# The low parts of the branch projections' weights: made by accumulating transfers in place of VectorE's subtraction

## The chip, the cores and the metric

One core of a Trainium2 chip runs the whole kernel. The metric is the device time of one execution in microseconds, as the median of the runs shown.

## The reference

One layer of a hybrid decoder, 256 rows of width 2048, all in float32. One input projection feeds three causal mixers (a gated linear recurrence, a windowed softmax attention, a short gated convolution). Each mixer's output `o_a`, `o_b`, `o_c` (256 x 1024) is projected to width 2048, weighted by a sigmoid gate that is itself a projection of the input, and the sum goes through one output projection and a layer norm:

```
u = x @ w_in[l]
...
y_a = (o_a.astype(x.dtype) * jax.nn.silu(a_g)) @ w_proj_hgrn[l]
...
y_b = (o_b * jax.nn.silu(b_g)) @ w_proj_attn[l]
...
y_c = (o_c * jax.nn.silu(c_g)) @ w_proj_conv[l]
merged = jax.nn.sigmoid(m_a) * y_a + jax.nn.sigmoid(m_b) * y_b + jax.nn.sigmoid(m_c) * y_c
y = merged @ w_out[l]
x = layer_norm(ALPHA * x + y, ln_g[l], ln_b[l])
```

The change lies in the weights of `y_a`, `y_b` and `y_c`.

## The kernel before

Every product is made from rounded operands in TensorE's float32r format. A weight `w` is split into a high part `hi`, which is `w` rounded to float32r, and a low part `lo = w - hi`; an activation is split the same way. A product is the sum of three matmuls: activation high by `hi` (L140), activation low by `hi` (L141), activation high by `lo` (L142). Columns-major products do the same with two instructions (L147, L148).

Weights come in granules of 1024 KB (128 partitions x 2048 numbers). `load_granule` (L103) takes one of three `raw` buffers and issues the load from SyncE's queue; a load waits until the buffer's last readers are done. `gemm` (L152) walks over the granules and splits each in two halves of 128 x 1024 with `split_w` (L108): ScalarE's copy writes `hi` (L111), VectorE's subtraction writes `lo` (L112). There are four `hi` and four `lo` buffers, so a half is split when TensorE has finished the half four places ahead of it. A half then feeds twelve matmuls of 128 x 512 in `rows` (L138), two k-steps by two row blocks by three.

The last third of the kernel is the loop over `d` (four column blocks of 512) and over the three branches. For each pair it makes the gate `rows512(mc + d)` (four granules, eight halves), its sigmoid `sg` on ScalarE (L630, one for each row block), then the branch projection `gemm(a[wp][d], outs[br], NC, "rows")` (two granules, four halves), and multiplies and adds with VectorE (L634, L635, L637). So a branch takes twelve halves, and there are twelve branches. After each `d` the merged block is transposed for the output projection (the task `turn`). The order on each engine is set by a scheduler that places instructions by the waits that it expects; GpSimd (POOL) has a queue of its own for transfers that it issues in software.

Of the kernel before, what the change touches and what calls it, by code (L numbers as in the profile page):

```python
# [10 lines left out]
F32R = mybir.dt.float32r  # L11
U8 = mybir.dt.uint8
AF = mybir.ActivationFunctionType
ALU = mybir.AluOpType
AX = mybir.AxisListType

P = 128
# [3 lines left out]
NC = 512  # L21
# [15 lines left out]
HALF = 1024  # L37
# [11 lines left out]
def hybrid_kernel(ctx, tc, a, out):  # L49
    nc = tc.nc  # L50
# [4 lines left out]
    hip = ctx.enter_context(tc.tile_pool(name="hip", bufs=4))  # L55
    lop = ctx.enter_context(tc.tile_pool(name="lop", bufs=4))
# [7 lines left out]
    def t8(shape, name, dt=F32):  # L64
        return w8.tile(shape, dt, tag="w8", name=name)

    def t4(shape, name, dt=F32):
        return w4.tile(shape, dt, tag="w4", name=name)
# [7 lines left out]
    def f32(ap):  # L76
        return ap.bitcast(F32)


    xs = [t8([P, 4, 2, T], f"xs{i}", F32R) for i in range(4)]  # L80

    def split_to(dst, src):

        nc.scalar.copy(out=dst[:, :, 0], in_=src)
        nc.vector.tensor_sub(out=dst[:, :, 1], in0=src, in1=f32(dst[:, :, 0]))

    def load_x(k0, n):
        xr = t4([P, n, T], f"xr{k0}")
        nc.sync.dma_start(out=xr, in_=a["xT"][:, k0 : k0 + n])
        return xs[k0 // 4][:, k0 % 4 : k0 % 4 + n], xr  # L90
# [4 lines left out]
    def pump(n=1):  # L95
        while n and tasks:
            try:
                next(tasks[0])
                n -= 1
            except StopIteration:  # L100
                tasks.pop(0)

    def load_granule(src):  # L103
        raw = rawp.tile([P, 2, HALF], F32, tag="raw", name="raw")
        nc.sync.dma_start(out=raw, in_=src.rearrange("p (s n) -> p s n", s=2))
        return raw

    def split_w(r, hi=None, lo=None):  # L108
        hi = hi if hi is not None else hip.tile([P, HALF], F32R, tag="hi", name="hi")
        lo = lo if lo is not None else lop.tile([P, HALF], F32R, tag="lo", name="lo")  # L110
        nc.scalar.copy(out=hi, in_=r)  # L111
        nc.vector.tensor_sub(out=lo, in0=r, in1=f32(hi))  # L112
        return hi, lo

    def first_granule(src, k0, pieces):

        raw = rawp.tile([P, 2 * HALF], F32, tag="raw", name="raw")
        loaded = []
        at = 0
        for n in pieces:  # L120
            x = load_x(k0 + at, n)
            c = slice(at * NC, (at + n) * NC)
            nc.sync.dma_start(out=raw[:, c], in_=src[:, c])
            loaded.append((x, c))
            at += n
        halves = []
        for x, c in loaded:
            split_to(*x)
            if c.start % HALF == 0:
                halves.append((hip.tile([P, HALF], F32R, tag="hi", name="hi"), lop.tile([P, HALF], F32R, tag="lo", name="lo")))  # L130
            w = slice(c.start % HALF, c.start % HALF + c.stop - c.start)
            split_w(raw[:, c], *[y[:, w] for y in halves[-1]])
        return halves

    def accumulators():
        return [accp.tile([P, NC], F32, tag="acc", name="acc") for _ in range(2)]

    def rows(acc, xk, hi, lo, ts, first, last):  # L138

        nc.tensor.matmul(out=acc, lhsT=xk[:, 0, ts], rhs=hi, start=first, stop=False)  # L140
        nc.tensor.matmul(out=acc, lhsT=xk[:, 1, ts], rhs=hi, start=False, stop=False)  # L141
        nc.tensor.matmul(out=acc, lhsT=xk[:, 0, ts], rhs=lo, start=False, stop=last)  # L142

    def columns(acc, xk, hi, lo, first, last):

        if not first:
            nc.tensor.matmul(out=acc[:, :T], lhsT=lo, rhs=xk[:, 0], start=False, stop=False)  # L147
        nc.tensor.matmul(out=acc, lhsT=hi, rhs=xk, start=first, stop=last)  # L148
        if first:
            nc.tensor.matmul(out=acc[:, :T], lhsT=lo, rhs=xk[:, 0], start=False, stop=False)  # L150

    def gemm(src, xs, n, major, first=None):  # L152


        acc = accumulators()
        per = HALF // n
        kt = src.shape[0] * 2 * per
        k = 0
        for g in range(src.shape[0]):
            if first:  # L160
                halves = first_granule(src[g], k, first[g])
            else:
                raw = load_granule(src[g])
            for s in range(2):
                hi, lo = halves[s] if first else split_w(raw[:, s])
                for j in range(per):
                    xk = xs[k // 4][:, k % 4]
                    for b in range(2):
                        c = slice(b * P, b * P + P)
                        if major == "rows":  # L170
                            w = slice(j * n, j * n + n)
                            rows(acc[b][:, :n], xk, hi[:, w], lo[:, w], c, k == 0, k == kt - 1)
                        else:
                            w = slice(j * n + b * P, j * n + b * P + P)
                            columns(acc[b], xk, hi[:, w], lo[:, w], k == 0, k == kt - 1)
                    k += 1
                pump()
        return acc

    def rows512(c, first=None):  # L180
        return gemm(a["w_rows"][c], xs, NC, "rows", first)

    def columns256(c):
        return gemm(a["w_cols"][c], xs, T, "columns")
# [359 lines left out]
    outs = {"a": [], "b": [], "c": []}  # L544
# [7 lines left out]
    first = ((1, 1, 2), (2, 2), (2, 2), (2, 2))  # L552

    for hf in range(2):
        v = rows_out(rows512(AI + hf, None if hf else first), "va")
        q = t4([P, 4, T], "qa")
        for u in range(2):
            acc = columns256(AQ + 2 * hf + u)
# [15 lines left out]
    conv(0)  # L574
    load_bias(C)
    acc = gemm(a["w_cols"][BV], xs, T, "rows")
    vb = t4([P, 2, 2, KVH * DH], "vb", F32R)
    vb = [vb[:, i] for i in range(2)]
# [3 lines left out]
    acc = columns256(BK)  # L582
# [5 lines left out]
    for w in range(2):  # L588
        r = slice(64 * w, 64 * w + 64)
        nc.scalar.copy(out=kz[0][r, :, w], in_=kr[r])  # L590
        nc.vector.tensor_sub(out=kz[1][r, :, w], in0=kr[r], in1=f32(kz[0][r, :, w]))
    for hf in range(2):
        gate = t4([P, 4, T], "gb")
        for u in range(2):
            acc = columns256(BG + 2 * hf + u)
# [5 lines left out]
        for u in range(2):  # L601
            acc = columns256(BQ + 2 * hf + u)
# [12 lines left out]
    def turn(m):  # L615
        dst = t8([P, 4, 2, T], "m", F32R)
        ms.append(dst)
        yield
        for i, ps in transpose_pairs([[m[:, t, c * P : c * P + P] for t in range(2)] for c in range(4)], "mT"):
            split_to(dst[:, i : i + 2], ps)  # L620
            yield

    branches = ((MA, "w_proj_hgrn", "a"), (MB, "w_proj_attn", "b"), (MC, "w_proj_conv", "c"))
    for d in range(4):
        m = t4([P, 2, NC], "merged")
        for n, (mc, wp, br) in enumerate(branches):
            acc = rows512(mc + d)
            sg = t4([P, 2, NC], "sg")
            for t in range(2):
                nc.scalar.activation(out=sg[:, t], in_=acc[t], func=AF.Sigmoid)  # L630
            acc = gemm(a[wp][d], outs[br], NC, "rows")
            for t in range(2):
                if n:
                    nc.vector.tensor_mul(out=sg[:, t], in0=acc[t], in1=sg[:, t])  # L634
                    nc.vector.tensor_add(out=m[:, t], in0=m[:, t], in1=sg[:, t])  # L635
                else:
                    nc.vector.tensor_mul(out=m[:, t], in0=acc[t], in1=sg[:, t])  # L637
        tasks.append(turn(m))
# [41 lines left out]
    for n in range(3):  # L680
        acc = gemm(a["w_out"][n], ms, NC, "rows")
# [3 lines left out]
    for g in range(4):  # L685
        raw = load_granule(a["w_out"][3, g])
# [7 lines left out]
    for t, at, n in ((0, 0, NC), (1, 0, T), (1, T, T)):  # L694
        acc = accp.tile([P, NC], F32, tag="acc", name="acc")[:, :n]
        for k in range(KT):
            hi, lo = parts[k // 2]
# [94 lines left out]
```

## Time and profile before

| | us |
|---|---|
| median of 2 runs | 1026.2 (1025.85 to 1026.55) |
| the profiled execution's own time | 1026.14 |
| its span, first to last instruction | 1024.3 |
| TensorE busy | 1009.3 |
| VectorE busy | 656.9 |
| ScalarE busy | 516.8 |
| GpSimd busy | 32.4 |

Matmul times overlap in the trace (one is listed with 0.39 us and the next starts 0.23 us behind it), so the pace of TensorE is read from the starts. "Idle before" in a group is the time in which the engine had nothing to do ahead of those instructions, and what ended it. A transfer's time "to landing" runs from its issue to the semaphore that tells of its end.

### The profile page before, as it was taken

To read this page: it belongs to the slowest core of one execution; us is meant where nothing else is said; L and a number is where in the kernel's file an instruction comes from. 1 tells how busy PE (TensorE), PEld (TensorE's weight loads), DVE (VectorE), ACT (ScalarE), POOL (GpSimd) and SP (SyncE) were. 2 spreads that over 40 slices of the span, in tenths; PEclk is the share of its full clock that TensorE was granted. 3 is DMA by queue.
4 is the path that set the end of the run, shared out by engine and by line. 5 is a ranking of instruction groups with operands and counts; after the bars stand their busy time and mean duration, and the time that the engine had idled before them with its cause. 6 is when DMAs were issued, how large, how long until landed. Compare 5 with 4: busy or idle time off the path is not lost.

```text
span 1024.3 us, 13046 instructions
## 1 busy us (share of the span) xinstructions
PE 1009.3 (99%) x5214; PEld 855.4 (84%) x5214; DVE 656.9 (64%) x810; ACT 516.8 (50%) x702; POOL 32.4 (3%) x32
## 2 busy tenths in 40 slices
PE   8999999999999999999999999999999999999995
PEld 5888888888988888888888888888888888888885
DVE  6557788689855777777764455545554555545666
ACT  5546577656564665646554434444444434444441
POOL 1000000210010000000000000000000000000003
PEclk9999999999999999999999999999999999999998
DMA  8655545354455545444455555555455556665442
GB/s 324 242 194 177 205 136 180 137 189 144 165 196 182 191 156 200 166 168 144 168 199 203 179 194 205 173 197 205 170 200 202 180 193 237 254 248 193 177 164 83
DMA packets 30253, 192.60 MB, mean 188 GB/s; under 512 B 3776, under 2 KB 4576, under 8 KB 8176
## 3 DMA queue, kind: packets, MB, share of 16 engines
q1 hardware_dynamic: 28368, 184.85, 50.9%
q10 hardware_dynamic: 1152, 4.72, 1.3%
q0 software_dynamic: 672, 2.20, 0.7%
q8 instruction: 41, 0.67, 0.3%
q14 instruction: 20, 0.16, 0.0%
HBM read 189.63 MB, written 2.12 MB: 187 GB/s over the span
## 4 chain that ended last, share of the span: by engine, by line
PE 97%; DMA 1%; DVE 1%; SPq 0%; ACT 0%; issue 0%
PE acc L148 24%; PE acc L142 19%; PE acc L140 19%; PE acc L141 19%; PE acc L147 11%; PE lev L385 1%; DMA raw<-in_w_rows 1%; PE sc L454 1%; PE pvb L497 1%; PE acc L150 1%; PE pT L487 1%; PE pv L406 0%; PE mT L259 0%; PE lev L375 0%; DVE xres L677 0%; DVE xres L675 0%
## 5 line engine op out<-in xcount | busy, mean ns | idle before, releaser
L112 DVE TENSOR_TENSOR lo<-raw,hi 128x1024 fp32r<-128x1024 f32 (+1 forms) x341 | 414.9, 1220 | 291.5 <-ACT hi L111 290.5
L111 ACT CAST hi<-raw 128x1024 fp32r<-128x1024 f32 (+1 forms) x341 | 356.7, 1048 | 388.2 <-PE acc L141 264.2
L148 PE MATMUL acc<-xs,hi 128*128 128x512 f32 x1056 | 371.9, 396 | 0.0
L147 PE MATMUL acc<-xs,lo 128*128 128x256 f32 x990 | 278.4, 281 | 0.0
L148 PEld LDWEIGHTS acc<-xs,hi 128*128 128x128 f32 x1056 | 197.0, 188 | 43.7
L140 PE MATMUL acc<-hi,xs 128*128 128x512 f32 (+1 forms) x544 | 210.5, 387 | 2.3 <-ACT hi L111 2.3
L142 PE MATMUL acc<-lo,xs 128*128 128x512 f32 (+1 forms) x544 | 208.4, 384 | 0.4 <-DVE lo L112 0.3
L141 PE MATMUL acc<-hi,xs 128*128 128x512 f32 (+1 forms) x544 | 208.7, 384 | 0.0
L147 PEld LDWEIGHTS acc<-xs,lo 128*128 128x128 f32 x990 | 186.8, 189 | 2.2
L140 PEld LDWEIGHTS acc<-hi,xs 128*128 128x128 f32 x544 | 102.5, 188 | 24.5 <-ACT hi L111 4.4
L142 PEld LDWEIGHTS acc<-lo,xs 128*128 128x128 f32 x544 | 102.2, 188 | 21.3 <-DVE lo L112 1.2
L141 PEld LDWEIGHTS acc<-hi,xs 128*128 128x128 f32 x544 | 102.6, 189 | 19.8
L188 ACT COPY rest<-acc 128x256 f32<-128x256 f32 x66 | 24.3, 373 | 46.2 <-PE acc L148 45.3
L140 PE MATMUL acc<-hi,m 128*128 128x512 f32 (+1 forms) x120 | 45.2, 376 | 0.0
L142 PE MATMUL acc<-lo,m 128*128 128x512 f32 (+1 forms) x120 | 45.0, 375 | 0.0
L141 PE MATMUL acc<-hi,m 128*128 128x512 f32 (+1 forms) x120 | 45.0, 375 | 0.0
L142 PEld LDWEIGHTS acc<-lo,m 128*128 128x128 f32 x120 | 22.6, 188 | 4.1
L140 PEld LDWEIGHTS acc<-hi,m 128*128 128x128 f32 x120 | 22.6, 188 | 4.0
L141 PEld LDWEIGHTS acc<-hi,m 128*128 128x128 f32 x120 | 22.6, 188 | 4.0
L140 PE MATMUL acc<-hi,oa 128*128 128x512 f32 x64 | 24.9, 389 | 0.0
L141 PE MATMUL acc<-hi,oa 128*128 128x512 f32 x64 | 24.9, 389 | 0.0
L142 PE MATMUL acc<-lo,oa 128*128 128x512 f32 x64 | 24.9, 389 | 0.0
(187 smaller groups left out, 912.1 us busy)
## 6 DMA issues: line engine op xcount, KB each, us to landing
raw<-in_w_cols SPq DMA_DIRECT2D x68, 1024.0 KB, 4.8
raw<-in_w_rows SPq DMA_DIRECT2D x60, 1024.0 KB, 4.7
raw<-in_w_out SPq DMA_DIRECT2D x16, 1024.0 KB, 4.8
raw<-in_w_proj_hgrn SPq DMA_DIRECT2D x8, 1024.0 KB, 4.7
raw<-in_w_proj_attn SPq DMA_DIRECT2D x8, 1024.0 KB, 4.7
raw<-in_w_proj_conv SPq DMA_DIRECT2D x8, 1024.0 KB, 4.7
raw<-in_w_rows SPq DMA_DIRECT2D x7, 512.0 KB, 8.9
bias<-bias_dr POOLq DMA_DIRECT2D x2, 1024.0 KB, 6.1
```

What stands on the lines that cost most here:

```text
L111: nc.scalar.copy(out=hi, in_=r)
L112: nc.vector.tensor_sub(out=lo, in0=r, in1=f32(hi))
L140: nc.tensor.matmul(out=acc, lhsT=xk[:, 0, ts], rhs=hi, start=first, stop=False)
L141: nc.tensor.matmul(out=acc, lhsT=xk[:, 1, ts], rhs=hi, start=False, stop=False)
L142: nc.tensor.matmul(out=acc, lhsT=xk[:, 0, ts], rhs=lo, start=False, stop=last)
L147: nc.tensor.matmul(out=acc[:, :T], lhsT=lo, rhs=xk[:, 0], start=False, stop=False)
L148: nc.tensor.matmul(out=acc, lhsT=hi, rhs=xk, start=first, stop=last)
L150: nc.tensor.matmul(out=acc[:, :T], lhsT=lo, rhs=xk[:, 0], start=False, stop=False)
L188: nc.scalar.copy(out=rest[p], in_=acc[p, T:])
L385: nc.tensor.matmul(out=ps[:, o : o + 64], lhsT=kk[:, hd, t * P : t * P + P], rhs=qc[:, hd, t * 64 : t * 64 + 64], start=True, stop=True)
L454: nc.tensor.matmul(out=ps[:, o_ : o_ + 2 * nk], lhsT=q[:, 2 * g + x, m, blk * P : blk * P + P], rhs=kz[n][:, hf, :, 0:nk], start=(i == 0), ...
L487: nc.tensor.transpose(out=ps[:, x * P : x * P + P], in_=s[:, x // 2, x % 2, j * P : j * P + P], identity=C["ident"])
```

## The change

In the twelve branch projections alone, `split_w` is replaced by `split_by_dma`. ScalarE writes the negated rounded weight into `lo`; a transfer issued by GpSimd then adds the raw weight onto it in place (raw and `lo` both lie in SBUF); ScalarE writes `hi` as before. All other products keep `split_w`. Lines behind the new function stand 9 lower than before.

```diff
+    def split_by_dma(r):
+
+        hi = hip.tile([P, HALF], F32R, tag="hi", name="hi")
+        lo = lop.tile([P, HALF], F32R, tag="lo", name="lo")
+        nc.scalar.mul(out=lo, in_=r, mul=-1.0)
+        nc.gpsimd.dma_start(out=lo, in_=r, accum_op=ALU.add)
+        nc.scalar.copy(out=hi, in_=r)
+        return hi, lo
...
-    def gemm(src, xs, n, major, first=None):
+    def gemm(src, xs, n, major, first=None, split=split_w):
...
-                hi, lo = halves[s] if first else split_w(raw[:, s])
+                hi, lo = halves[s] if first else split(raw[:, s])
...
-            acc = gemm(a[wp][d], outs[br], NC, "rows")
+            acc = gemm(a[wp][d], outs[br], NC, "rows", split=split_by_dma)
```

Two places show how the instructions stand. The first is ScalarE at the first attention projection (d = 0): four halves, with the two sigmoids of its gate between them. Before:

```order
L111 CAST hi_5281<-raw_5279 128x1024 [waits DMAHW1_49,DVE_49,PE_49]
L111 CAST hi_5297<-raw_5279 128x1024 [waits DVE_49,PE_49]
L111 CAST hi_5315<-raw_5313 128x1024 [waits DMAHW2_49,DVE_49,PE_49]
L630 ACTIVATE sg_5274<-acc_5136 128x512 [waits PE_49]
L111 CAST hi_5331<-raw_5313 128x1024 [waits DVE_49,PE_49]
L630 ACTIVATE sg_5274<-acc_5137 128x512 [waits PE_49]
L111 CAST hi_5355<-raw_5353 128x1024 [waits DMAHW3_49,DVE_49,PE_49]
```

Each half has one instruction here; VectorE takes the rest of its split. ScalarE there in the changed kernel, where `lo` (L119) is the new multiplication by -1 and the names' numbers are four higher:

```order
L121 CAST hi_5285<-raw_5283 128x1024 [waits DMAHW1_49,DVE_49,PE_49]
L119 ACTIVATE lo_5286<-raw_5283 128x1024 [waits DMASW6_49,PE_49]
L121 CAST hi_5302<-raw_5283 128x1024 [waits DVE_49,PE_49]
L119 ACTIVATE lo_5303<-raw_5283 128x1024 [waits DMASW7_49,PE_49]
L121 CAST hi_5321<-raw_5319 128x1024 [waits DMAHW2_49,DVE_49,PE_49]
L119 ACTIVATE lo_5322<-raw_5319 128x1024 [waits DMASW0_49,PE_49]
L639 ACTIVATE sg_5278<-acc_5140 128x512 [waits PE_49]
L121 CAST hi_5338<-raw_5319 128x1024 [waits DVE_49,PE_49]
L639 ACTIVATE sg_5278<-acc_5141 128x512 [waits PE_49]
L119 ACTIVATE lo_5339<-raw_5319 128x1024 [waits DMASW1_49]
L111 CAST hi_5363<-raw_5361 128x1024 [waits DMAHW3_49,PE_49,Activation_49]
```

The new instruction stands behind the half's `hi`; that of the fourth half stands behind both sigmoids, and `hi` of the next half (`hi_5363`) behind that.

The second place is SyncE's queue there: the two granules of the projection and the three that follow. Before, the loads wait for VectorE (DVE) as the last reader of the buffer:

```order
L105 DMA raw_5279<-in_w_proj_attn 128x2048 [waits DMAHW6_49,DVE_49]
L105 DMA raw_5313<-in_w_proj_attn 128x2048 [waits DMAHW7_49,DVE_49]
L105 DMA raw_5353<-in_w_rows 128x2048 [waits DMAHW0_49,DVE_49]
L105 DMA raw_5387<-in_w_rows 128x2048 [waits DMAHW1_49,DVE_49]
L105 DMA raw_5421<-in_w_rows 128x2048 [waits DMAHW2_49,DVE_49]
```

All five wait for the same two kinds of event. In the changed kernel the loads that take over the projection's two buffers wait for accumulating transfers instead (DMASW is the software queue's semaphore):

```order
L105 DMA raw_5283<-in_w_proj_attn 128x2048 [waits DMAHW6_49,DVE_49]
L105 DMA raw_5319<-in_w_proj_attn 128x2048 [waits DMAHW7_49,DVE_49]
L105 DMA raw_5361<-in_w_rows 128x2048 [waits DMAHW0_49,DVE_49]
L105 DMA raw_5395<-in_w_rows 128x2048 [waits DMASW3_49,DMAHW1_49,DMASW2_49,Activation_49]
L105 DMA raw_5429<-in_w_rows 128x2048 [waits DMASW5_49,DMAHW2_49,DMASW4_49,Activation_49]
```

`raw_5395` and `raw_5429`, the loads behind the projection's granules, no longer wait for VectorE but for two accumulating transfers each. On GpSimd nothing stood between the second bias transfer of the attention (L435) and the layer norm (L667); the 48 transfers `lo<-raw` stand there now, in the order of the halves.

## Rows read from the trace of the kernel before

**Rows 1.** The page of the kernel before: busy time, and the chain that ended last.
```profile
PE 1009.3 (99%) x5214; PEld 855.4 (84%) x5214; DVE 656.9 (64%) x810; ACT 516.8 (50%) x702; POOL 32.4 (3%) x32
...
PE 97%; DMA 1%; DVE 1%; SPq 0%; ACT 0%; issue 0%
```

**Rows 2.** Stretches of the span: busy time by engine, granted clock, share of DMA engines, GB/s.
```profile
core 0: us, PE busy (x) PEld busy (x) DVE busy (x) ACT busy (x) POOL busy (x), PEclk, DMA share, GB/s
0.00:545.00 545.00, 540.87 (x3089) 465.89 (x3090) 398.97 (x552) 320.10 (x492) 23.71 (x24) 1.00 0.52 184
545.00:900.00 355.00, 355.00 (x1579) 293.89 (x1578) 184.72 (x172) 149.71 (x157) 0.00 (x0) 1.00 0.57 201
900.00:1024.00 124.00, 113.40 (x550) 95.66 (x548) 73.16 (x87) 46.96 (x53) 8.67 (x8) 0.97 0.47 169
```

**Rows 3.** Groups of ScalarE in the branch projections' stage, 545 to 900 us.
```profile
L111 ACT CAST hi<-raw 128x1024 fp32r<-128x1024 f32 x129 | 135.9, 1053 | 190.8 <-PE acc L141 189.1 <-DVE lo L112 1.7
L630 ACT ACTIVATE sg<-acc 128x512 f32<-128x512 f32 x22 | 13.2, 598 | 13.3 <-PE acc L142 13.3
```

**Rows 4.** Groups of VectorE in 560 to 900 us, different shapes apart.
```profile
L112 DVE TENSOR_TENSOR lo<-raw,hi 128x1024 fp32r<-128x1024 f32 x124 | 151.9, 1225 | 159.8 <-ACT hi L111 159.8
```

**Rows 5.** ScalarE in order of time around the first attention projection (576 to 590 us).
```profile
start us, us, engine line op out<-in xcount [idle before <-releaser]
...
576.21 1.05 ACT L111 CAST hi<-raw 128x1024 fp32r<-128x1024 f32 x1 [1.67 <-PE acc L141]
578.93 1.05 ACT L111 CAST hi<-raw 128x1024 fp32r<-128x1024 f32 x1 [1.67 <-PE acc L141]
581.65 1.05 ACT L111 CAST hi<-raw 128x1024 fp32r<-128x1024 f32 x1 [1.67 <-PE acc L141]
583.91 0.60 ACT L630 ACTIVATE sg<-acc 128x512 f32<-128x512 f32 x1 [1.21 <-PE acc L142]
584.41 1.04 ACT L111 CAST hi<-raw 128x1024 fp32r<-128x1024 f32 x1
585.35 0.60 ACT L630 ACTIVATE sg<-acc 128x512 f32<-128x512 f32 x1
587.09 1.05 ACT L111 CAST hi<-raw 128x1024 fp32r<-128x1024 f32 x1 [1.14 <-PE acc L141]
```

**Rows 6.** TensorE in order of time there: where the projection's first half begins.
```profile
576.01 0.39 PE L142 MATMUL acc<-lo,xs 128*128 128x512 f32 x1
576.24 0.39 PE L140 MATMUL acc<-hi,xs 128*128 128x512 f32 x1
...
584.17 0.39 PE L142 MATMUL acc<-lo,xs 128*128 128x512 f32 x1
584.40 0.39 PE L140 MATMUL acc<-hi,ob 128*128 128x512 f32 x1
584.62 0.39 PE L141 MATMUL acc<-hi,ob 128*128 128x512 f32 x1
584.85 0.39 PE L142 MATMUL acc<-lo,ob 128*128 128x512 f32 x1
...
587.57 0.39 PE L142 MATMUL acc<-lo,ob 128*128 128x512 f32 x1
```

**Rows 7.** One weight load of 1024 KB: its issue, and DMA in 575.8 to 580.8 us (40 slices).
```profile
575.83 5.77 SPq L105 DMA_DIRECT2D raw<-in_w_rows  x2
...
DMA  0000000590409019199691996939499440000000
...
q1 hardware_dynamic: 144, 1.05, 59.6%
...
raw<-in_w_rows SPq DMA_DIRECT2D x1, 1024.0 KB, 4.7
```

**Rows 8.** VectorE's low parts and the loads that they release, in order of time.
```profile
577.29 1.23 DVE L112 TENSOR_TENSOR lo<-raw,hi 128x1024 fp32r<-128x1024 f32 x1 [1.50 <-ACT hi L111]
580.02 1.23 DVE L112 TENSOR_TENSOR lo<-raw,hi 128x1024 fp32r<-128x1024 f32 x1 [1.50 <-ACT hi L111]
582.74 1.23 DVE L112 TENSOR_TENSOR lo<-raw,hi 128x1024 fp32r<-128x1024 f32 x1 [1.49 <-ACT hi L111]
585.48 1.23 DVE L112 TENSOR_TENSOR lo<-raw,hi 128x1024 fp32r<-128x1024 f32 x1 [1.52 <-ACT hi L111]
...
581.27 0.33 SPq L105 DMA_DIRECT2D raw<-in_w_rows  x1
```

**Rows 9.** The software queue's 1024 KB transfer (bias), issued at 300.22 us: DMA share by stretch.
```profile
300.22 0.96 POOL L435 DMA_DIRECT2D bias<-bias_dr  x1
...
300.20:301.70 1.50, 1.50 (x11) 1.29 (x10) 1.41 (x6) 0.30 (x1) 0.97 (x2) 1.00 0.00 0
301.70:303.00 1.30, 1.30 (x11) 1.17 (x10) 1.30 (x4) 0.78 (x1) 0.00 (x0) 1.00 0.74 205
303.00:306.30 3.30, 3.30 (x22) 2.89 (x22) 3.09 (x5) 1.95 (x5) 0.00 (x0) 1.00 1.03 364
```

**Rows 10.** The page of the kernel before: DMA issues, size of one, median us from issue to landing.
```profile
raw<-in_w_proj_hgrn SPq DMA_DIRECT2D x8, 1024.0 KB, 4.7
...
bias<-bias_dr POOLq DMA_DIRECT2D x2, 1024.0 KB, 6.1
...
oh<-in_onehot POOLq DMA_DIRECT2D x1, 48.0 KB, 3.1
...
rb<-in_rel_bias POOLq DMA_DIRECT2D x1, 2.0 KB, 3.1
```

## The prediction

> **What bounds the kernel now.** I read the page's busy times first, then the stretches of the span, then the engines in order of time around one branch projection. The page shows TensorE busy for 1009.3 of 1024.3 us and the chain that ended last made of TensorE for 97% [rows 1]. The stretches show that the branch projections' stage has no gap at all: 355.00 us busy of 355, at a granted clock of 1.00, with VectorE at 184.7 us, ScalarE at 149.7 us and the DMA engines at 0.57 [rows 2]. So nothing that VectorE is spared can shorten this stage: a gain is excluded, and the only question is whether the new `lo` comes late.
>
> In order of time, `hi` of a half is written 8.2 us ahead of its first matmul: 576.21 us for the half that TensorE begins at 584.40 [rows 5, 6]. That lead is three halves of TensorE's time, since a half can be split only when the half four places ahead of it has left its buffer (its last matmul with `lo` starts at 576.01 us [rows 6]). One half takes TensorE 2.72 us, the distance between the first `lo` matmuls of two halves, 584.85 and 587.57 [rows 6]. ScalarE works 1.05 us of each 2.72 and waits 1.67 for TensorE [rows 5].
>
> **The change part by part.**
>
> *Removed:* 48 subtractions (12 projections x 2 granules x 2 halves) of 1225 ns [rows 4], 58.8 us of VectorE. It has 170 us idle in the stage; worth 0.
>
> *Added on ScalarE:* 48 multiplications of 128x1024 into float32r. The nearest row is the cast of the same shape, 1053 ns [rows 3], so 50.5 us of ScalarE against 205 us idle. By halves: 2.1 us of each 2.72, and at the fourth half two sigmoids of 0.60 us besides [rows 5]. The next half's `hi` starts at 587.09 us now; my times below end ScalarE's work at 587.05, so it is not delayed. Worth 0. If the multiplication took twice as long, about 1 us of the lead would go.
>
> *Added on GpSimd:* 48 transfers. GpSimd has nothing else in the stage (0.00 us busy [rows 2]); the one software transfer of 1024 KB kept it 0.96 us [rows 9], under the 2.72 between two halves. Nothing useful is queued behind a transfer that waits.
>
> *Added on the DMA engines:* 48 x 512 KB, summed in place. The trace has no such transfer. I put its time from issue to landing as 1.5 + s + 0.6 us. The 1.5 is the software transfer's stretch from its issue to the first byte, in which the DMA share is 0.00 [rows 9]. The 0.6 is the weight load's tail: issued at 575.83, its last busy slice ends at 579.9 and it lands 4.7 us after the issue [rows 7]. s is the time in which the 16 engines move the half. A load of 1024 KB fills them for 59.6% of 5.0 us = 2.98 us [rows 7]. So the bounds of s are 1.5 us, if adding costs what copying 512 KB costs, and 4.5 us, if reading both operands and writing one cost three passes one after the other. I take **s = 3.0 us**: in a load, reading and writing the same bytes overlap, and the adding transfer has to read two streams of 512 KB, as many bytes as a load.
>
> A price by a page alone: the Trainium skill, in "Collectives: The Full Stack", section "The bandwidth ceiling: the fold count and why AG ≠ RS ≠ AR", says that the adding step runs at half the copying one's rate since it reads two sources (62.28 against 32.35 GB/s, a ratio of 1.93). By it s would be an estimated 2.9 us and the time an estimated 1053 us; no run here shows it yet.
>
> Now the four halves of the projection at 584.40 us, by the order in the changed kernel (`hi`, then the multiplication, then the transfer):
>
> First half: `hi` from 576.21, multiplied by 578.3, transfer issued. Bytes move 579.8 to 582.8; the load issued at 575.83 is off the engines by 579.9 [rows 7]. Landed 583.4. TensorE wants this `lo` at 584.85 [rows 6]: 1.4 us to spare.
>
> Second half: `hi` at 578.93 [rows 5], issue 581.1, bytes 582.6 to 585.7, landed 586.3, wanted at 587.57: 1.3 us to spare.
>
> Here the first granule's buffer comes free, and SyncE issues the load that waits for it, at 586.3; before it was issued at 581.27, behind VectorE's subtraction of 580.02 [rows 8]. Its bytes start 0.9 us later (the seven empty slices of 0.125 us in [rows 7]), at 587.2, and need 3.0 us of the engines.
>
> Third half: `hi` at 581.65, issue 583.8, bytes from 585.3. Wanted at 584.85 + 2 x 2.72 = 590.29.
>
> Fourth half: `hi` at 584.41 between the sigmoids, sigmoid until 585.95 [rows 5], multiplied by 587.0, issue 587.05, bytes from 588.5. Wanted at 593.01.
>
> From 585.3 on the engines never rest: 0.4 us are left of the second half, then 3.0 of the third, 3.0 of the load, 3.0 of the fourth. While the software transfer and a load ran together in 303.0 to 306.3 us they moved 364 GB/s at a share of 1.03 [rows 9], no more than 1.05 MB in 2.98 us, or 352 GB/s [rows 7], so they share and do not add. All is moved at 585.3 + 9.4 = 594.7, and the fourth half, begun last, lands at 595.3. TensorE waits 595.3 - 593.0 = **2.3 us per projection** (part of it at the third half already; the total is the same).
>
> Do the later loads add to it? The load issued at 586.3 has landed by 595.3 at the latest. The cast that needs it ran two halves behind 587.09 [rows 5], at 592.5, and moves by under 3 us; TensorE wants that half at 584.40 + 6 x 2.72 = 600.7, and cast and subtraction take 2.3 us. The load behind the fourth half is issued at 595.3 and lands by about 601; its half is wanted at 606.2. Both hold, so each projection starts afresh after eight halves of its gate.
>
> **Sum:** 12 x 2.3 = 27.6 us. Against the profiled execution's own 1026.14 us (span 1024.3; the median of the runs is 1026.2, the same within 0.1) that is **1054 us**, 2.7% slower. Under 2% either way (about 20 us) counts as no change here.
>
> **The rivals.**
>
> *Hidden.* The adding transfer costs what a copy does, s = 1.5: the second half lands at 584.7, the load's bytes run from 585.6, the fourth half's bytes from 588.5 share with the load's last 1.2 us and are through at 591.3, landed 591.9 against 593.01. No wait: 1026 us. Working the same sum at s = 2.0 gives 592.9, so the rival holds up to there; a small wait, under 2% in all, holds to about s = 2.8. For it: 0.43 of the DMA engines' time is free in the stage [rows 2], and an adder in the data's way need not slow it. Against: two operands have to be read. The Trainium skill, "DMA: Bandwidth & Descriptors", section "Anatomy of one DMA — SWDGE (gpsimd) path", gives 2.0 us plus the bytes at 436 GB/s for a software transfer: an estimated 3.2 us for a half, and by that rule nothing waits and the time stays at an estimated 1026 us. The only plain software transfer here, 1024 KB in 6.1 us beside a load [rows 9, 10], is slower than the 4.4 us of that rule.
>
> *Overrun.* Summing is slower than reading, s = 4.5 or more. Then the transfers queue behind each other, since one comes each 2.72 us: from 579.8 the engines owe 4 x 4.5 + 3.0 = 21.0 us, done at 600.8, landed 601.4, a wait of 8.4 us per projection: 12 x 8.4 = 101 us, 1127 us. At s = 6 it is 14.4 per projection, 1199 us. For it: nothing in the trace shows how fast the engines add. Against: an adding step that keeps pace with its reads needs no more than 3.0.
>
> *It does not do what it says*, as the transfer might be broken up or a subtraction stay. The order shows 48 whole transfers of 128x1024 and no VectorE subtraction in the projections, so I leave it 2 in 100.
>
> **How the numbers follow.** Forecast (s from 2.0 to 3.8) 0.44, hidden 0.27, overrun 0.27, other 0.02. The range reaches from the hidden case, 1025, to the overrun at s = 4.5, 1130, and leaves out the longer overruns. Of the forecast's cases about a quarter (s under 2.8) stays within 2%: same 0.27 + 0.11 = 0.38; slower 0.60; faster 0.02, for which I know no mechanism.
>
> **What the profile after would show.** Right: 48 transfers on the software queue of 512 KB that land in 5 to 8 us, the fourth of each projection later than the first; about 28 us of TensorE idle in the stage, at the line of the `lo` matmul (L151 there), released by a transfer, two per projection at most; the weight loads behind a projection issued some 5 us later; ScalarE's multiplication at 1.05 us. Wrong: landings under 4.5 us and no idle time (hidden), or landings over 8 us that grow through the four halves (overrun). It would also be wrong if the granted clock fell after the waits, or if the weight loads and not `lo` became late.

## The result and the profile after

The changed kernel takes 1084.9 us (median of 2 runs, 1083.4 to 1086.3) against 1026.2 us before: a ratio of 1.057, with a 95% interval of 1.054 to 1.060. It is 58.7 us slower. The profiled execution took 1083.38 us, with a span of 1081.6. (A ratio is taken over the executions within 1.5% of the same kernel's fastest; for the fifth experiment below, whose times scatter, it is therefore smaller than the ratio of the medians.)

The page of the changed kernel, with the lines that answer to [rows 1] and [rows 10], and the groups that are new:

```profile
span 1081.6 us, 13234 instructions
...
PE 1030.7 (95%) x5214; PEld 867.4 (80%) x5214; DVE 598.8 (55%) x762; ACT 562.1 (52%) x750; POOL 73.9 (7%) x80
...
PEclk9999999999999999999999999999999999899998
DMA  8655544453554554445588688778778778996542
...
PE 63%; issue 16%; DMA 16%; DVE 2%; POOL 2%; ACT 0%; SPq 0%; POOLq 0%; ACTq 0%; DVEq 0%
...
L120 POOL DMA_DIRECT2D lo<-raw x48 | 41.5, 865 | 530.8 <-ACT lo L119 502.3
...
L119 ACT ACTIVATE lo<-raw 128x1024 fp32r<-128x1024 f32 x48 | 50.7, 1056 | 0.0
...
L151 PE MATMUL acc<-lo,ob 128*128 128x512 f32 x64 | 28.3, 441 | 12.6 <-DMA lo<-raw 12.6
L151 PE MATMUL acc<-lo,oc 128*128 128x512 f32 x64 | 27.3, 427 | 11.9 <-DMA lo<-raw 11.9
L151 PE MATMUL acc<-lo,oa 128*128 128x512 f32 x64 | 27.2, 425 | 11.4 <-DMA lo<-raw 11.4
...
lo<-raw POOLq DMA_DIRECT2D x48, 512.0 KB, 5.0
```

TensorE is busy for 1030.7 us where it was for 1009.3, with the same 5214 instructions, and idle for 1081.6 - 1030.7 = 50.9 us where it was for 15.0. So of the 57.3 us by which the span grew, **35.9 us are idle time, and for 21.4 us the same instructions are busy for longer**. VectorE is relieved by 58.1 us (656.9 to 598.8) and the multiplication costs ScalarE 1056 ns each, close to the 1053 forecast. The chain, 97% TensorE before, has 16% of DMA and 16% of "issue" in it. The three groups of `lo` matmuls of the projections carry the idle time, 11.4 to 12.6 us each, put down to the transfers; these sum to the 35.9 us. The transfers' median landing is 5.0 us: I had forecast 5.1 for one that shares with nothing.

The branch projections' stage by stretches, answering to [rows 2]: the granted clock is 0.96 where it was 1.00, and the DMA engines' share 0.79 where it was 0.57.

```profile
core 0: us, PE busy (x) PEld busy (x) DVE busy (x) ACT busy (x) POOL busy (x), PEclk, DMA share, GB/s
...
545.00:900.00 355.00, 327.73 (x1389) 266.64 (x1387) 113.39 (x110) 169.37 (x179) 34.61 (x40) 0.96 0.79 224
```

In order of time, around the projection that [rows 5, 6 and 8] show before. It begins 4.82 us later here (589.22 in place of 584.40), since one projection has been through already. GpSimd's four transfers, the load that the second one's landing releases, and TensorE at the fourth half:

```profile
583.33 0.86 POOL L120 DMA_DIRECT2D lo<-raw  x1 [27.89 <-ACT lo L119]
586.05 0.86 POOL L120 DMA_DIRECT2D lo<-raw  x1 [1.86 <-ACT lo L119]
588.77 0.86 POOL L120 DMA_DIRECT2D lo<-raw  x1 [1.86 <-ACT lo L119]
592.01 0.86 POOL L120 DMA_DIRECT2D lo<-raw  x1 [2.37 <-PE acc L150]
```

```profile
591.29 0.33 SPq L105 DMA_DIRECT2D raw<-in_w_rows  x1
```

```profile
597.60 0.39 PE L150 MATMUL acc<-hi,ob 128*128 128x512 f32 x1
601.17 0.50 PE L151 MATMUL acc<-lo,ob 128*128 128x512 f32 x1 [3.17 <-DMA lo<-raw]
...
602.39 0.63 PE L149 MATMUL acc<-hi,ob 128*128 128x512 f32 x1
602.82 0.63 PE L150 MATMUL acc<-hi,ob 128*128 128x512 f32 x1
...
605.38 0.39 PE L150 MATMUL acc<-hi,xs 128*128 128x512 f32 x1
605.61 0.40 PE L151 MATMUL acc<-lo,xs 128*128 128x512 f32 x1
```

The four transfers landed 4.9, 5.1, 5.0 and **9.1 us** after their issues at 583.33 to 592.01. The load went out at 591.29, 5.2 us later against TensorE's course than the 581.27 of [rows 8]. So the fourth transfer, issued 0.7 us behind the load, landed at 601.1, and the matmul that wants its `lo` at 597.83 started at 601.17. Then the matmuls follow each other by 0.43 us in place of 0.23, for some 3.5 us. The stretches say why: the DMA engines are full up to 598, TensorE does nothing from 598.0 to 601.1, and the granted clock of the next stretch is 0.61, a mean of 1.00 at its start and the lower of the two levels (0.50, 1.2 GHz) behind it.

```profile
589.20:598.00 8.80, 8.79 (x39) 6.94 (x37) 2.45 (x2) 4.61 (x6) 1.30 (x2) 1.00 1.00 223
598.00:601.10 3.10, 0.00 (x0) 0.00 (x0) 1.23 (x1) 1.04 (x1) 0.00 (x0) 1.00 0.58 114
601.10:605.00 3.90, 3.83 (x11) 3.02 (x12) 0.69 (x1) 0.18 (x1) 0.00 (x0) 0.61 0.67 231
```

What the engines moved meanwhile, 591 to 602 us:

```profile
DMA  9999499794879999989976799999999410000000
...
q0 software_dynamic: 257, 0.92, 45.2%
q1 hardware_dynamic: 144, 1.05, 34.6%
...
lo<-raw POOLq DMA_DIRECT2D x1, 512.0 KB, 9.1
```

The software queue filled the 16 engines for 45.2% of these 11 us and the loads' queue for 34.6%: 8.8 us of work on all engines between 591 and 600, for the rest of the third transfer, the load and the fourth. The load's 1.05 MB took 3.8 us of that (34.6% of 11; 3.8 to 4.2 by the packets of all twelve projections); alone they took 2.98 [rows 7]. The two queues hardly mixed here. From 593.5 to 596.5 us the view of the DMA queues lists the loads' queue alone:

```profile
q1 hardware_dynamic: 103, 0.84, 99.2%
```

The load's first bytes moved at 593.1, when the third transfer was nearly through, and the fourth transfer's at 596.9, when the load was. That is 4.9 us after its issue, and 4.3 to 5.2 in the twelve projections; the first three transfers' bytes moved 1.4 to 1.7 us after theirs.

All twelve projections look like this: first, second and third transfers land in 4.5 to 6.0 us, the fourth in 8.4 to 9.9, and TensorE pauses once in each, for 2.45 to 3.98 us. With ten of the twelve pauses the clock fell. One of these ten stretches at the lower level, and the sum over all ten:

```profile
601.96:605.37 3.41, 3.41 (x9) 2.64 (x8) 0.87 (x2) 0.55 (x1) 0.00 (x0) 0.50 0.86 305
...
sum 37.52, PE 36.35 PEld 28.46 DVE 12.03 ACT 4.79 POOL 0.00; mean PE 3.63 PEld 2.85 DVE 1.20 ACT 0.48 POOL 0.00
```

TensorE was busy for 36.35 us at half the clock, so the clock cost about 18.2 of the 21.4 us. Of the rest some 2 us come from the counting: before a pause a matmul counts with its listed 0.39 us and not with the 0.23 to the next start, which is 12 x 0.16. The last 1.3 us were not assigned.

### The profile page after: what moved, and what is told of

Same layout as the page of the kernel before. It is cut to its first block, busy times and chain, and to the rows that moved or that the text cites. A ratio compares the mean times of both kernels' runs of the same rounds, so it can differ in the third digit from the quotient of the medians.

```text
span 1081.6 us, 13234 instructions
## 1 busy us (share of the span) xinstructions
PE 1030.7 (95%) x5214; PEld 867.4 (80%) x5214; DVE 598.8 (55%) x762; ACT 562.1 (52%) x750; POOL 73.9 (7%) x80
## 4 chain that ended last, share of the span: by engine, by line
PE 63%; issue 16%; DMA 16%; DVE 2%; POOL 2%; ACT 0%; SPq 0%; POOLq 0%; ACTq 0%; DVEq 0%
PE acc L157 23%; PE acc L156 11%; DMA lo<-raw 10%; PE acc L151 9%; PE acc L149 8%; PE acc L150 8%; DMA raw<-in_w_proj_attn 2%; DMA raw<-in_w_proj_hgrn 2%; POOL lo L120 2%; DMA raw<-in_w_proj_conv 1%; DVE lo L112 1%; PE lev L394 1%; PE sc L463 1%; PE pvb L506 1%; PE acc L159 1%
## 5 line engine op out<-in xcount | busy, mean ns | idle before, releaser
L112 DVE TENSOR_TENSOR lo<-raw,hi 128x1024 fp32r<-128x1024 f32 (+1 forms) x293 | 356.0, 1219 | 367.7 <-ACT hi L111 366.8
L111 ACT CAST hi<-raw 128x1024 fp32r<-128x1024 f32 (+1 forms) x293 | 305.9, 1047 | 374.1 <-PE acc L150 215.8
L149 PEld LDWEIGHTS acc<-hi,xs 128*128 128x128 f32 x544 | 104.0, 191 | 25.1 <-ACT hi L111 4.0
L151 PEld LDWEIGHTS acc<-lo,xs 128*128 128x128 f32 x544 | 103.2, 190 | 21.4 <-DVE lo L112 0.9
L150 PEld LDWEIGHTS acc<-hi,xs 128*128 128x128 f32 x544 | 103.6, 191 | 20.4
L120 POOL DMA_DIRECT2D lo<-raw x48 | 41.5, 865 | 530.8 <-ACT lo L119 502.3
L121 ACT CAST hi<-raw 128x1024 fp32r<-128x1024 f32 x48 | 50.4, 1051 | 37.0 <-PE acc L150 37.0
L119 ACT ACTIVATE lo<-raw 128x1024 fp32r<-128x1024 f32 x48 | 50.7, 1056 | 0.0
L149 PE MATMUL acc<-hi,m 128*128 128x512 f32 (+1 forms) x120 | 45.2, 376 | 0.0
L151 PE MATMUL acc<-lo,ob 128*128 128x512 f32 x64 | 28.3, 441 | 12.6 <-DMA lo<-raw 12.6
L151 PE MATMUL acc<-lo,oc 128*128 128x512 f32 x64 | 27.3, 427 | 11.9 <-DMA lo<-raw 11.9
L151 PE MATMUL acc<-lo,oa 128*128 128x512 f32 x64 | 27.2, 425 | 11.4 <-DMA lo<-raw 11.4
```

Source lines behind the costliest of these rows:

```text
L119: nc.scalar.mul(out=lo, in_=r, mul=-1.0)
L120: nc.gpsimd.dma_start(out=lo, in_=r, accum_op=ALU.add)
```

## The experiments

All are made from the changed kernel. Theory A: an adding transfer fills the engines about twice as long as a copy, and the fourth of a projection has to share them with the weight load that the second one's landing releases (in the changed kernel it waits behind it); the pause this makes brings the clock down. Theory B puts the cost in the software queue itself, theory C in the late issue of the fourth transfer.

**e1_copy: transfers that do not add.** `lo` holds the raw weight here; the addition is left out.

```diff
-        nc.gpsimd.dma_start(out=lo, in_=r, accum_op=ALU.add)
+        nc.gpsimd.dma_start(out=lo, in_=r)
```

> The transfer copies the raw weight over lo without adding, so the addition is left out and the low parts hold raw weights; the instructions, their order and their waits stay. Theory A (the engines are filled by the adding transfers' second read, and the fourth one of a projection shares them with the weight load that the second one releases): one transfer fills the engines for about 1.5 us in place of 2.8, lands in 3.6 to 4.5 us, the fourth in under 5.8, TensorE does not wait and the clock stays at 1.00: 1026 to 1031 us. Theory B (the cost is in the software queue or in the conversion to float32r, whatever the arithmetic): landings stay at 5 us and at 9 us for the fourth: 1078 to 1088 us.

Measured: 1030.7 us, 1.004 times the kernel before (1.003 to 1.005). The software queue's line of the page, of the kernel before, of the changed kernel and of this one, and the transfers' line here:

```profile
q0 software_dynamic: 672, 2.20, 0.7%
```

```profile
q0 software_dynamic: 7584, 27.37, 13.1%
```

```profile
q0 software_dynamic: 7584, 27.37, 7.6%
...
lo<-raw POOLq DMA_DIRECT2D x48, 512.0 KB, 3.8
```

The changed kernel and this one have the same packets and bytes, and this one the smaller share. In the kernel before, whose software transfers [rows 10] are in both of these too, the queue took 0.7% of 1024.3, or 7.2 us of all engines. So 48 adding transfers filled them for 141.7 - 7.2 = 134.5 us, **2.80 us each**, and 48 copies for 78.1 - 7.2 = 70.9 us, **1.48 each**. I had taken 3.0 and 1.5. Theory B falls: the same queue with the same conversion costs 4 us in all when it need not add. In this run the third transfer meets the load, and lands after 5.7 to 7.9 us in eight of twelve projections; it had time to spare, and three short pauses are left, 2.1 us in all.

**e2_hold: the loads behind a projection wait for its fourth transfer.** Nothing else is changed; GpSimd copies one column of the fourth `lo` into the `raw` buffer that the load will fill.

```diff
-    def load_granule(src):
+    def load_granule(src, hold=False):
         raw = rawp.tile([P, 2, HALF], F32, tag="raw", name="raw")
+        if hold and last_lo:
+            nc.gpsimd.tensor_copy(out=raw[:, 0, :1], in_=f32(last_lo[-1][:, :1]))
+            held.append(raw)
+            if len(held) % 2 == 0:
+                last_lo.clear()
...
-                raw = load_granule(src[g])
+                raw = load_granule(src[g], g in (1, 2) and split is split_w)
```

> The two weight loads behind a projection also wait, by a one-column copy on GpSimd, for the projection's fourth adding transfer. Theory A (sharing with the load makes the fourth transfer late): the fourth lands about 5 to 6 us after its issue in place of 9.1, TensorE waits under 0.5 us for lo, and the held loads land some 2 us before TensorE would need them: 1026 to 1036 us. Theory C (the fourth is late since it is issued late, behind the sigmoids, and queues behind the three before it): it still lands after 8 to 9 us, and the held loads come later still: 1085 us or more.

Measured: 1029.3 us, ratio 1.002 (1.001 to 1.003). All 48 adding transfers stay. The transfers' landings and the stage by stretches:

```profile
DMA to landing us min/median/max: 4.5/4.7/6.3
```

```profile
545.00:900.00 355.00, 355.00 (x1579) 293.78 (x1578) 128.75 (x127) 189.87 (x202) 41.30 (x66) 1.00 0.86 261
```

The fourth transfers land after 4.5 to 5.9 us, TensorE has no idle time in these 355 us (one pause of 1.25 us is left, in the last projection), and the clock is 1.00. The fourth is issued as late as in the changed kernel, behind the same sigmoids, so theory C falls too. The held loads come late for ScalarE, which waits up to 7.0 us for them, but not for TensorE. This one wait on two loads gives back 55.5 of the 58.7 us.

**e3_fill: work in the pause.** Fourteen extra matmuls, whose results nobody reads, stand ahead of the first `lo` matmul of each fourth half.

```diff
         nc.tensor.matmul(out=acc, lhsT=xk[:, 1, ts], rhs=hi, start=False, stop=False)
+        if fill:
+            ps = bank("fill")
+            for _ in range(fill):
+                nc.tensor.matmul(out=ps, lhsT=xk[:, 1, ts], rhs=hi, start=True, stop=True)
```

> In each projection's fourth half 14 extra matmuls of 128x512 into a spare bank stand ahead of the first matmul that needs lo, so TensorE works through most of the 3.3 us in which it waited; the extra work adds nothing to the result. If the fall of the clock follows from TensorE's pause: granted clock 1.00 in the stage, the pause is replaced by 14 x 0.227 = 3.2 us of work, and the 1.7 us per projection at half clock go: 1026 + 12 x 3.4 = 1064 to 1072 us. If the clock falls for another reason (the transfers' traffic, say): the clock stays at 0.95 in the stage and the time at 1083 us or more.

Measured: 1072.5 us, ratio 1.044 (1.042 to 1.046): **12.4 us faster than the changed kernel, with 168 matmuls more**. By stretches:

```profile
545.00:900.00 355.00, 351.01 (x1553) 288.46 (x1552) 117.16 (x114) 171.89 (x181) 34.51 (x40) 1.00 0.81 229
```

The granted clock is 1.00 with the transfers, the load and the late fourth landing all still there (9.8 and 11.3 us in the first two projections of this run). So it is TensorE's pause that brings the clock down, not the traffic. Of the pauses 4.2 us are left, where the transfer landed later still. This prices the clock a second time: 31.7 us of pause are gone, 168 x 0.227 = 38.1 us of work have come, and the time is 12.4 us shorter, so 18 to 19 us must have come back from the clock.

**e4_lolast: the fourth half's `lo` matmuls at its end.** The same products, in another order.

```diff
+                if split is split_by_dma and (g, s) == (1, 1):
+                    for part in range(2):
+                        for j in range(per):
+                            xk = xs[(k + j) // 4][:, (k + j) % 4]
+                            for b in range(2):
...
+                                if part:
+                                    nc.tensor.matmul(out=y, lhsT=xk[:, 0, c], rhs=lo[:, w], start=False, stop=j == per - 1)
+                                else:
+                                    nc.tensor.matmul(out=y, lhsT=xk[:, 0, c], rhs=hi[:, w], start=False, stop=False)
+                                    nc.tensor.matmul(out=y, lhsT=xk[:, 1, c], rhs=hi[:, w], start=False, stop=False)
```

> In each projection's fourth half the eight matmuls with hi go first and the four with lo last, so lo is wanted 6 x 0.227 = 1.36 us later; the sums are the same. Theory A: the fourth transfer lands when it did, the pause shrinks from 3.3 to about 1.9 us. If the clock falls as before, 12 x 1.36 = 16 us come back: 1069 us. If a pause of 1.9 us leaves the clock at 1.00, 12 x 1.7 = 21 us more come back: 1049 us.

Measured: 1057.6 us, ratio 1.031 (1.027 to 1.035), between the two cases. The twelve pauses sum to 20.4 us where they summed to 35.9: 15.5 us less, as expected. They are 0.9 to 2.8 us long. Two of them with the stretch behind each, one of 2.59 us (to 635.5) and one of 1.73 us (to 706.6):

```profile
632.95:635.45 2.50, 0.00 (x0) 0.00 (x0) 0.67 (x1) 1.74 (x2) 0.00 (x0) 1.00 0.15 28
635.50:639.00 3.50, 3.50 (x9) 2.79 (x10) 2.56 (x5) 0.20 (x1) 0.00 (x0) 0.54 0.66 225
704.90:706.55 1.65, 0.00 (x0) 0.00 (x0) 1.23 (x1) 1.26 (x2) 0.00 (x0) 1.00 0.18 35
706.60:710.00 3.40, 3.40 (x15) 2.83 (x16) 2.41 (x5) 0.00 (x0) 0.00 (x0) 1.00 0.65 219
```

Behind the first the clock is 0.54, behind the second 1.00. It fell with two pauses of the twelve, those of 2.59 and 2.79 us, so most of the clock's loss came back as well.

**e5_vneg: the negated weight written by VectorE**, which waits neither for `hi` nor for the sigmoids.

```diff
-        nc.scalar.mul(out=lo, in_=r, mul=-1.0)
+        nc.vector.tensor_scalar_mul(lo, r, -1.0)
```

> VectorE in place of ScalarE writes the negated rounded weight, so it neither waits behind the half's hi nor, in the fourth half, behind the two sigmoids: the first three transfers go out some 0.9 us earlier, the fourth some 1.5 us. Theory A (the fourth shares the engines with the weight load that the second one's landing releases): that load moves forward with them, so the two still meet, the fourth takes 8 to 9 us, and the pause shrinks from 3.0 to about 1.5 to 2 us; the clock then mostly stays at 1.00: 1044 to 1052 us. Theory C (it is late only since it is issued late): it lands after 5 us, no pause, 1026 to 1031 us.

Measured: 1067.7 us (median of 4, from 1049.2 to 1075.8; ratio 1.028, 1.022 to 1.035). Theory A's forecast is missed: the profiled execution, the slowest of the four, has pauses of 0.7 to 4.0 us that sum to 31.1, though the fourth transfer is issued 2.72 us behind the third in place of 3.24, and all four sooner. The loads' queue in the first 2.5 us from the first transfer's issue, here and in the changed kernel:

```profile
q1 hardware_dynamic: 106, 0.87, 85.3%
...
lo<-raw POOLq DMA_DIRECT2D x1, 512.0 KB, 5.8
```

```profile
q1 hardware_dynamic: 86, 0.57, 54.7%
...
lo<-raw POOLq DMA_DIRECT2D x1, 512.0 KB, 4.9
```

Issued sooner, the first transfer meets the load ahead of it, which fills the engines for 85% of that time in place of 55%; it lands after 5.8 us in place of 4.9, and the fourth after 8.3 to 11.6. The engines' work is the same and starts no sooner.

The packets show that the twelve projections of this trace are of two kinds. In seven the fourth transfer's first byte moved 5.8 to 5.9 us after its issue, when the load was nearly through, and TensorE paused for 2.7 to 4.0 us. In five it moved 2.0 to 2.1 us after its issue, beside the load's bytes, and TensorE paused for 0.7 to 2.2 us. In the seven the load had been issued 0.29 to 0.53 us behind the fourth transfer, in the five 0.56 to 1.54 us behind it. So the length of the pause goes with whether the transfer's bytes move beside the load's or behind them. The queues in the 4 us from the load's first byte, in a projection of the first kind and in one of the second:

```profile
q1 hardware_dynamic: 108, 0.88, 93.6%
q0 software_dynamic: 19, 0.02, 2.5%
```

```profile
q1 hardware_dynamic: 93, 0.76, 54.0%
q0 software_dynamic: 102, 0.39, 50.7%
```

The four executions, from 1075.8 and 1074.6 over 1060.7 to 1049.2 us, have mean granted clocks of 0.980, 0.980, 0.987 and 0.994 (0.994 to 0.997 before). From 0.994 to 0.980 is 1.4% of the time, so some 15 of the 27 us by which they scatter are the clock. A changing share of the two kinds could make both parts, but no trace of the quicker executions was kept, and this is not shown.

**e7_only4 and e8_not4: one transfer per projection, or three.** In the first only the fourth half goes by an adding transfer, in the second all but the fourth; the others keep VectorE's subtraction.

```diff
-                hi, lo = halves[s] if first else split(raw[:, s])
+                hi, lo = halves[s] if first else (split if (g, s) == (1, 1) else split_w)(raw[:, s])
```

(with `!=` in the second).

> Only the fourth half of each projection goes by a transfer, 12 in all; the other three by VectorE's subtraction. The transfer is issued as late as before, but the weight load behind the second half goes out some 5 us earlier, as in the kernel before. Theory A: nothing shares with the transfer, it lands after 4.5 to 5 us, TensorE does not wait: 1026 to 1029 us. Theory C (late issue): it is late still, a pause of 2 us or more in each projection: 1050 us or more.

> The first three halves of each projection go by transfers, 36 in all, the fourth by VectorE's subtraction. Theory A: the load that the second transfer's landing releases meets the third transfer's tail at most, which had 4 us to spare in the changed kernel; no pause: 1026 to 1030 us. If each transfer costs TensorE something by itself (by SBUF traffic beside the matmuls, say), three quarters of the 58 us stay: about 1070 us.

Measured: 1026.9 us, ratio 1.0005 (0.9996 to 1.0014), and 1026.6 us, ratio 1.001 (1.000 to 1.002). The landings of the twelve, then those of the thirty-six:

```profile
DMA to landing us min/median/max: 4.5/4.5/5.2
```

```profile
DMA to landing us min/median/max: 4.5/4.9/6.5
```

Neither has a pause. The fourth transfer by itself, issued just as late, lands after 4.5 us. Three of four transfers cost nothing, so a transfer has no price of its own for TensorE: nearly all of the 58.7 us hang on the fourth coming behind the load (e2_hold) with three others ahead of both. The fourth and the load without those three were not run.

## Why the prediction was right and wrong

*Right: no gain.* With TensorE busy 355 of 355 us, the 58 us taken from VectorE bought nothing; e8_not4 takes 36 x 1.225 = 44 of them without a pause, and stays at 1026.6.

*Right: the price of adding.* s was taken as 3.0 us between 1.5 and 4.5; it measured 2.80, and the copy 1.48. The Trainium skill, "Collectives: The Full Stack", section "The bandwidth ceiling: the fold count and why AG ≠ RS ≠ AR", gives a ratio of 1.93 between a collective that copies and one that adds, for reading two sources; the traces here, of transfers inside one core, agree with 2.80 / 1.48 = 1.89. (The prediction's own sum gives about 1050 us for the s of 2.9 that it took from there, not 1053.) The other rule of the Trainium skill that was weighed, in "DMA: Bandwidth & Descriptors", section "Anatomy of one DMA — SWDGE (gpsimd) path", gave an estimated 3.2 us for a half. That lies among the copies (2.9 us at best, 3.8 in the median) but not among the adding transfers, whose quickest took 4.5 us.

*Right: the place.* One pause per projection, at the fourth half, through the load that the second landing releases. Its issue came 5.2 us later than before (forecast 5), the first three transfers landed in time, and the later loads did not add to it: TensorE's idle time in the stage is all at the three groups of `lo` matmuls. The landings, forecast at 5 to 8 us, were 4.5 to 6.0 us and, for the fourth, 8.4 to 9.9.

*Wrong, first: the fall of the clock had no price.* The last lines name it ("It would also be wrong if the granted clock fell after the waits"), but the sum, 12 x 2.3 = 27.6 us, took TensorE at 1.00 throughout. Twelve pauses brought it to the lower level ten times, and about 18 of the 57.3 us are that. e3_fill shows the cause: with work in the pause the clock stays at 1.00. This is the step that failed.

*Wrong, second, by size: the term of 2.3 us per projection.* It measured 35.9 / 12 = 3.0 us. The fourth transfer was to land 8.25 us after its issue (587.05 to 595.3) and took 8.4 to 9.9. The sum had 9.4 us of work for the engines from the third transfer on (0.4 + 3.0 + 3.0 + 3.0); by the packets it was 9.6, as medians of the twelve, but otherwise made up: the load took 3.9 in place of 3.0, and the transfers 5.7 in place of 6.4. With the measured s of 2.80 the same sum would have given only about 1.6 us, so an s set a little high made up in part for a load set too low. Another 0.3 us is at the end: the sum allowed 0.6 us from the last byte to the landing, and the trace has about 0.9 us without work, counting the engines that run dry behind 599.5 (the last digits above). The rest, some 0.2 us, was not assigned. So 27.6 us became 35.9.

Together 28 us were forecast and 58.7 measured. That this lies inside the stated range is luck: the range reached so far for the sake of the overrun case, and that case (transfers slower than their reads) did not happen.

## What to carry to other kernels

Taking work from an engine that is off the path buys nothing, and the transfer that replaces it draws on a resource that has a chain of its own: add up the time that each transfer fills the DMA engines, an adding one as nearly two copies (1.89 here), over the stretch in which its result is wanted, and look for the load that its landing releases, since a transfer issued around that load can wait for the whole of it. A pause of TensorE is dearer than its length: here 3.0 us cost about 4.5 (35.9 and 18.2 us over twelve), so a wait of a few us should be priced with the clock behind it. Where such a transfer stays, holding back a load that has time to spare (e2_hold) was worth more than issuing the transfer sooner (e5_vneg).

## What the runs showed of the hardware

TensorE's clock fell to the lower level with pauses of 2 to 4 us in a kernel that is otherwise busy without a gap. In the changed kernel it fell with ten pauses of 2.52 to 3.98 us (in three of them up to 0.7 us before the pause ended) and not with those of 2.45 and 2.52 us. In e4_lolast it fell with those of 2.59 and 2.79 us and with none of the ten of 0.9 to 2.1 us. In e5_vneg it fell behind one of 2.16 us, while one of 2.16 us in e3_fill left it at 1.00. So the length of the pause alone does not tell it.

When an adding transfer and a load meet, the order of their bytes sets the price. In the projection shown the fourth transfer's bytes waited for the load's, so the load landed after 7.35 us in place of 4.8, and the transfer after 9.1 in place of the 4.5 that it takes by itself (e7_only4). The load's bytes filled the engines for 3.8 us in place of 2.98, though for 3 us of that no other queue had a share. In e5_vneg a load ahead of a waiting transfer took 3.8 to 4.3 us of the engines, and one whose bytes moved beside the transfer's 2.6 to 2.9. Why a load with a transfer waiting behind it takes longer, and what decides which of the two goes first, was not tested.
